# A decoder layer on one core: each pair of heads gets its transposes, its values and the next pair's scores in one place of the TensorE order, at nine steps

## The chip, the cores and the metric

One core of one Trainium2 chip runs the whole layer. The metric is the device time of one execution in microseconds (us), as the median of several executions. Before the change it is 853.51 us (three runs, 853.31 to 853.89).

## The reference, cut to what matters

The layer projects x (512 tokens, 1024 channels, float32) to queries, keys and values of three dilation groups with 8 heads of 64, to the input of a state-space branch and to gates. Each group attends causally over a window; the groups are merged by their softmax denominators, both branches are projected and gated, and a normalisation, a SwiGLU layer and another normalisation follow.

```python
q = apply_rope(q, pos); k = apply_rope(k, pos)
for g, (window, dilation) in enumerate(((128, 1), (512, 4), (2048, 16))):
    o_g, lse_g = dilated_group_attention(q[:, :, g], k[:, :, g], v[:, :, g], window, dilation)
    ...
wts = jax.nn.softmax(jnp.stack(lses, axis=0), axis=0)
attn = jnp.sum(wts[..., None] * jnp.stack(outs, axis=0), axis=0)
```

## The kernel before

Every dense product is made of three matmuls (`mm3`, lines 187 to 190): both operands are split in a high and a low part, and high by high, high by low and low by high are added in PSUM. The projection is a list of 56 tiles, `STEPS`; a tile is 24 matmuls of 128x128 by 128x512. Steps 4 to 7 make the values of group 0, 8 to 19 gates, 20 to 27 keys and queries of group 0, 28 to 39 group 1, 40 to 51 group 2 (k, q, v, k, q), and 52 to 55 the last four gate tiles. After them come the GLU (line 1035 on), the branch projections, the output projection and the feed-forward part.

Other work is put between these tiles by hand. `at_step(n, fn, ...)` files a call under a step, and `run_fill(n)` makes the calls filed there in the order of filing. A whole n is run in the middle of tile n (`mid`, between its 12th and 13th matmul), and n + 0.5 is run after tile n and after `w.release()`. That release emits the split of the next weights into the slot just freed: a cast to the high part on ScalarE (ACT, line 181), a subtraction for the low part on VectorE (DVE, line 182) and, every second time, the load of the next raw weights on SyncE (SP, line 118). Each engine works through its own instructions in the order in which the program emits them.

Attention is done for two kinds (0: group 0; 1: groups 1 and 2 together) and four pairs of heads each, in three functions:

- `attn_scores` (from line 785): the scores of four blocks of queries on TensorE (PE, line 799) into four PSUM banks; then for each block and head DVE masks them and takes the maximum (line 810) and ACT takes the exponential (line 812), into a tile `un` per block.
- `attn_turn` (line 815 on): for each block PE transposes `un` (line 822: 14 transposes for a pair of kind 0, 16 for kind 1) into a bank, and ACT copies it back into `un` (line 824).
- `attn_values` (line 826 on): PE multiplies `un` with the values (line 833: 28 matmuls for kind 0, 32 for kind 1), and ACT copies the result (lines 839 and 841).

Scores and values of neighbouring pairs stand together at nine places (`SCORES`), and the transposes stand alone at eight places in between (`WEIGHTS`). For the pairs that the prediction names: the transposes of pair 0 of kind 0 are at 32, its values and the scores of pair 1 at 33.5; the transposes of pair 3 of kind 1 are at 54, its values at 55.5.

Around the end of this stage `merge_weights` computes the weights of the merge from the maxima and denominators of all pairs: three small operations on DVE, an exponential on ACT (line 872), five small operations on DVE, a cast to `wt` on ACT (line 879) and a last subtraction on DVE. `merge_turn` transposes `wt` on PE (line 885). `split_y` splits the state-space result for the GLU: four operations on ACT (line 184) and four on DVE (line 185). None of the three issues a DMA. `merge_near` (SP and POOL) and `merge_sel` (DVE) keep their steps.

Of the kernel before, what the change touches and what calls it, by code (L numbers as in the profile page):

```python
# [44 lines left out]
NLAST = 4  # L45


SCORES = [[30, 33.5, 37, 40, 43.5], [43.5, 48.5, 51.5, 53, 55.5]]
WEIGHTS = [[32, 35.5, 38.5, 42], [45, 50, 52.5, 54]]

# [101 lines left out]
def emit(ctx, tc, i, out):  # L154
# [71 lines left out]
    for n in range(2, N_GLU, 2):  # L226
        kind, g, un, _ = STEPS[n]
# [699 lines left out]
    def at_step(n, fn, *a):  # L927
        fill.setdefault(n, []).append((fn, a))
# [37 lines left out]
        at_step(28 + rnd, ssm_out, rnd)  # L966
    at_step(30, turn_y)
    for kind in range(2):
        for j, n in enumerate(SCORES[kind]):
            if j > 0:  # L970
                at_step(n, attn_values, kind, j - 1)
            if j < NPAIR:
                at_step(n, attn_scores, kind, j)
                at_step(WEIGHTS[kind][j], attn_turn, kind, j)
    xn = []
    pending = []

# [12 lines left out]
    at_step(43, merge_near, 0)  # L990
    at_step(45, merge_near, 1)
    at_step(52, merge_sel)
    at_step(54.5, split_y)
    at_step(54, merge_weights)
    at_step(55.5, merge_turn)
    for hp in range(NPAIR):
        at_step((58, 59, 60, 61)[hp], merge_pair, hp)

# [11 lines left out]
    for n in range(4, N_GLU):  # L1010
        kind, g, un, c = STEPS[n]
# [345 lines left out]
def build(inputs):  # L1357
    import concourse.bacc as bacc

    a = {k: np.asarray(v) for k, v in inputs.items()}  # L1360
    arrays = {f"in_{k}": np.ascontiguousarray(v) for k, v in {**layout(a), **constants()}.items()}
    nc = bacc.Bacc("TRN2", target_bir_lowering=False, num_devices=1)
    aps = {k[3:]: nc.dram_tensor(k, v.shape, mybir.dt.from_np(v.dtype), kind="ExternalInput").ap()
           for k, v in arrays.items()}
    out = nc.dram_tensor("out_dram", (S, D), F32, kind="ExternalOutput").ap()
    with tile.TileContext(nc) as tc:
        with ExitStack() as ctx:
            with tc.manual_schedule():
                emit(ctx, tc, aps, out)
    return nc, arrays  # L1370
# [8 lines left out]
```

## Time and profile before

| | |
|---|---|
| median of the runs | 853.51 us (853.31 to 853.89) |
| the profiled execution | 853.05 us, of which its span is 851.3 us |
| PE busy | 842.9 us (99%) |
| ACT busy | 302.8 us (36%) |
| DVE busy | 485.4 us (57%) |

The profile shows one execution. The span runs from the first to the last instruction, and 1.75 us lie around it. Ends of matmuls are modelled, so what a matmul takes of PE's time is read from one start to the next.

### The profile page before, as it was taken

To read this page: it belongs to the slowest core of one execution; us is meant where nothing else is said; L and a number is where in the kernel's file an instruction comes from. 1 tells how busy PE (TensorE), PEld (TensorE's weight loads), DVE (VectorE), ACT (ScalarE), POOL (GpSimd) and SP (SyncE) were. 2 spreads that over 40 slices of the span, in tenths; PEclk is the share of its full clock that TensorE was granted. 3 is DMA by queue.
4 is the path that set the end of the run, shared out by engine and by line. 5 is a ranking of instruction groups with operands and counts; after the bars stand their busy time and mean duration, and the time that the engine had idled before them with its cause. 6 is when DMAs were issued, how large, how long until landed. Compare 5 with 4: busy or idle time off the path is not lost.

```text
span 851.3 us, 11306 instructions
## 1 busy us (share of the span) xinstructions
PE 842.9 (99%) x4576; PEld 702.2 (82%) x4576; DVE 485.4 (57%) x949; ACT 302.8 (36%) x481; POOL 25.4 (3%) x27
## 2 busy tenths in 40 slices
PE   9999999999999999999999999999999999999996
PEld 7888888888888888888888898888888888888885
DVE  7977899964666446347785854433434434222237
ACT  6873221264344444643241332222222222211101
POOL 0000000000000000000000500000000000000005
PEclk9999999999999999999999999999999999999999
DMA  9822421424121321121642142222222222422203
GB/s 331 208 99 88 124 99 54 145 79 170 50 99 50 102 100 50 50 95 55 247 146 102 50 149 99 99 99 99 99 100 99 93 89 89 136 94 97 97 0 100
DMA packets 24580, 90.06 MB, mean 106 GB/s; under 512 B 6352, under 2 KB 11216, under 8 KB 15440
## 3 DMA queue, kind: packets, MB, share of 16 engines
q1 hardware_dynamic: 22752, 86.59, 29.7%
q10 hardware_dynamic: 1776, 2.74, 0.9%
q8 instruction: 36, 0.59, 0.3%
q14 instruction: 16, 0.13, 0.0%
HBM read 84.87 MB, written 4.46 MB: 105 GB/s over the span
## 4 chain that ended last, share of the span: by engine, by line
PE 98%; DMA 1%; DVE 0%; SPq 0%; issue 0%; DVEq 0%; ACT 0%
PE fg L188 9%; PE fg L190 9%; PE fg L189 9%; PE dn L190 4%; PE dn L189 4%; PE dn L188 4%; PE pg L188 4%; PE pg L189 3%; PE pg L190 3%; PE pv L188 3%; PE pk L188 3%; PE pq L188 3%; PE pv L189 3%; PE pv L190 3%; PE pq L190 3%; PE pk L190 3%
## 5 line engine op out<-in xcount | busy, mean ns | idle before, releaser
L182 DVE TENSOR_TENSOR wlo<-raw,whi 128x1024 fp32r<-128x1024 f32 x134 | 164.3, 1227 | 192.5 <-ACT whi L181 192.5
L181 ACT CAST whi<-raw 128x1024 fp32r<-128x1024 f32 x134 | 140.1, 1047 | 234.9 <-PE dn L190 73.4
L188 PE MATMUL fg<-hh,whi 128*128 128x512 f32 (+1 forms) x376 | 141.4, 376 | 0.0
L189 PE MATMUL fg<-hl,whi 128*128 128x512 f32 (+1 forms) x376 | 141.3, 376 | 0.0
L190 PE MATMUL fg<-hh,wlo 128*128 128x512 f32 (+1 forms) x376 | 141.3, 376 | 0.0
L189 PEld LDWEIGHTS fg<-hl,whi 128*128 128x128 f32 x376 | 70.8, 188 | 12.9
L190 PEld LDWEIGHTS fg<-hh,wlo 128*128 128x128 f32 x376 | 70.8, 188 | 12.9
L188 PEld LDWEIGHTS fg<-hh,whi 128*128 128x128 f32 x376 | 70.8, 188 | 12.6
L189 PE MATMUL dn<-wlo,ff 128*128 128x512 f32 x168 | 65.4, 389 | 0.0
L190 PE MATMUL dn<-whi,ff 128*128 128x512 f32 x168 | 65.4, 389 | 0.0
L188 PE MATMUL dn<-whi,ff 128*128 128x512 f32 x168 | 65.4, 389 | 0.0
L188 PE MATMUL pg<-x_hi,whi 128*128 128x512 f32 x128 | 50.5, 395 | 0.0
L184 ACT ACTIVATE ff<-fth 128x512 fp32r<-128x512 f32 x22 | 14.0, 634 | 102.8 <-DVE fth L321 102.8
L190 PE MATMUL pg<-x_hi,wlo 128*128 128x512 f32 x128 | 49.9, 390 | 0.0
L189 PE MATMUL pg<-x_lo,whi 128*128 128x512 f32 x128 | 49.9, 390 | 0.0
L321 DVE TENSOR_TENSOR fth<-fth,fg 128x512 f32<-128x512 f32 x22 | 15.1, 688 | 56.8 <-PE fg L190 56.7
L188 PE MATMUL pq<-x_hi,whi 128*128 128x512 f32 x96 | 37.9, 395 | 0.0
L188 PE MATMUL pk<-x_hi,whi 128*128 128x512 f32 x96 | 37.8, 394 | 0.0
L190 PE MATMUL pq<-x_hi,wlo 128*128 128x512 f32 x96 | 37.5, 390 | 0.0
L190 PE MATMUL pk<-x_hi,wlo 128*128 128x512 f32 x96 | 37.4, 390 | 0.0
L189 PE MATMUL pq<-x_lo,whi 128*128 128x512 f32 x96 | 37.4, 390 | 0.0
L189 PE MATMUL pk<-x_lo,whi 128*128 128x512 f32 x96 | 37.4, 390 | 0.0
(256 smaller groups left out, 1460.4 us busy)
## 6 DMA issues: line engine op xcount, KB each, us to landing
raw<-in_w_in SPq DMA_DIRECT2D x26, 1024.0 KB, 4.8
raw<-in_w_gu SPq DMA_DIRECT2D x22, 1024.0 KB, 4.7
raw<-in_w_dn SPq DMA_DIRECT2D x11, 1024.0 KB, 4.7
raw<-in_w_br SPq DMA_DIRECT2D x4, 1024.0 KB, 4.8
raw<-in_w_out SPq DMA_DIRECT2D x4, 1024.0 KB, 4.7
raw<-in_w_glu SPq DMA_DIRECT2D x2, 1024.0 KB, 4.7
xn<-in_x SPq DMA_DIRECT2D x2, 1024.0 KB, 7.9
out_dram<-hn SPq DMA_DIRECT2D x12, 128.0 KB, 2.3
```

The lines of the kernel that those rows point to most:

```text
L181: act.copy(hi, src)
L182: dve.tensor_tensor(lo, src, hi.bitcast(F32), op=ALU.subtract)
L184: act.mul(hi, src, scale)
L188: pe.matmul(dst, a[0], b[0], start=first, stop=False)
L189: pe.matmul(dst, a[0], b[1], start=False, stop=False)
L190: pe.matmul(dst, a[1], b[0], start=False, stop=last)
L321: eng.tensor_tensor(o, a, b, op=op)
```

## The change

`SCORES` and `WEIGHTS` become one list, `TURNS`. At each of its steps the transposes of the pair before, its values and the scores of the next pair are emitted one behind the other. All steps of the list are whole, so every place lies in the middle of a tile. `split_y`, `merge_weights` and `merge_turn` move by half a step to a step.

```diff
-SCORES = [[30, 33.5, 37, 40, 43.5], [43.5, 48.5, 51.5, 53, 55.5]]
-WEIGHTS = [[32, 35.5, 38.5, 42], [45, 50, 52.5, 54]]
+TURNS = [[30, 33, 36, 39, 43], [43, 48, 51, 53, 55]]
...
     for kind in range(2):
-        for j, n in enumerate(SCORES[kind]):
+        for j, n in enumerate(TURNS[kind]):
             if j > 0:
+                at_step(n, attn_turn, kind, j - 1)
                 at_step(n, attn_values, kind, j - 1)
             if j < NPAIR:
                 at_step(n, attn_scores, kind, j)
-                at_step(WEIGHTS[kind][j], attn_turn, kind, j)
...
     at_step(52, merge_sel)
-    at_step(54.5, split_y)
-    at_step(54, merge_weights)
-    at_step(55.5, merge_turn)
+    at_step(53.5, split_y)
+    at_step(54.5, merge_weights)
+    at_step(55, merge_turn)
```

## Rows read from the trace of the kernel before

**Rows 1.** The page, its first two parts: busy time of the engines, then the granted clock in 40 slices.
```profile
PE 842.9 (99%) x4576; PEld 702.2 (82%) x4576; DVE 485.4 (57%) x949; ACT 302.8 (36%) x481; POOL 25.4 (3%) x27
...
PEclk9999999999999999999999999999999999999999
```
**Rows 2.** The page's chain that ended last, by engine.
```profile
PE 98%; DMA 1%; DVE 0%; SPq 0%; issue 0%; DVEq 0%; ACT 0%
```
**Rows 3.** Who PE waited for, whole span: total us, times, longest.
```profile
PE warm_b L267 <- DVE warm L263: 1.1, 1, 1.1
PE pu L595 <- ACT wuh L181: 0.3, 1, 0.3
```
**Rows 4.** PE in order of time around the transposes at step 32: start, length, instruction.
```profile
198.21 0.39 PE L190 MATMUL pk<-x_hi,wlo 128*128 128x512 f32 x1
198.44 1.69 PE L822 MATMUL t<-ident,un 128*128 128x128 f32 x14
199.89 0.48 PE L188 MATMUL pk<-x_hi,whi 128*128 128x512 f32 x1
...
200.43 0.39 PE L190 MATMUL pk<-x_hi,wlo 128*128 128x512 f32 x1
```
**Rows 5.** PE around the values and scores at step 33.5, the same columns.
```profile
207.92 0.39 PE L190 MATMUL pk<-x_hi,wlo 128*128 128x512 f32 x1
208.24 1.75 PE L833 MATMUL o<-un,v 128*64 128x128 f32 x28
209.91 1.79 PE L799 MATMUL s<-k,q 64*128 64x128 f32 x16
211.63 0.50 PE L188 MATMUL pk<-x_hi,whi 128*128 128x512 f32 x1
```
**Rows 6.** PE around the transposes at step 54 (kind 1).
```profile
356.66 0.40 PE L190 MATMUL pg<-x_hi,wlo 128*128 128x512 f32 x1
356.90 1.91 PE L822 MATMUL t<-ident,un 128*128 128x128 f32 x16
358.56 0.47 PE L188 MATMUL pg<-x_hi,whi 128*128 128x512 f32 x1
...
359.11 0.40 PE L190 MATMUL pg<-x_hi,wlo 128*128 128x512 f32 x1
```
**Rows 7.** PE from the first matmul of tile 55 on: its 1st, its 13th, its last, and the place at 55.5.
```profile
361.41 0.39 PE L188 MATMUL pg<-x_hi,whi 128*128 128x512 f32 x1
...
364.13 0.39 PE L188 MATMUL pg<-x_hi,whi 128*128 128x512 f32 x1
...
366.94 1.97 PE L833 MATMUL o<-un,v 128*64 128x128 f32 x32
368.84 0.66 PE L885 MATMUL wt<-ident,wt 128*128 128x128 f32 x4
```
**Rows 8.** PE at step 53: the values of a pair of kind 1, then the scores.
```profile
347.43 1.97 PE L833 MATMUL o<-un,v 128*64 128x128 f32 x32
349.33 2.06 PE L799 MATMUL s<-k,q 64*128 64x128 f32 x32
```
**Rows 9.** ACT in order of time: the copies at step 32, four merged in one row; in brackets the idle time before and what ended it.
```profile
198.91 2.00 ACT L824 COPY un<-t 128x256 f32<-128x256 f32 x4 [1.46 <-PE t L822]
```
**Rows 10.** ACT from step 54 to the first GLU tile.
```profile
357.59 2.05 ACT L824 COPY un<-t 128x512 f32<-128x512 f32 x4 [0.94 <-PE t L822]
359.50 0.29 ACT L872 ACTIVATE dm<-dm 128x64 f32<-128x64 f32 x1
361.03 0.24 ACT L879 CAST wt<-dm 128x64 fp32r<-128x64 f32 x1 [1.24 <-DVE dm L321]
361.61 0.69 ACT L912 ACTIVATE gt<-pg,bgate 128x512 f32<-128x512 f32 x1 [0.34 <-PE pg L190]
362.20 1.04 ACT L181 CAST whi<-raw 128x1024 fp32r<-128x1024 f32 x1
```
**Rows 11.** DVE in the same stretch.
```profile
357.83 0.18 DVE L321 TENSOR_TENSOR mg<-near_st,st 128x32 f32<-128x32 f32 x1
...
358.16 0.18 DVE L321 TENSOR_TENSOR dm<-mg,st 128x32 f32<-128x32 f32 x1
359.82 0.19 DVE L321 TENSOR_TENSOR mg<-dm,near_st 128x32 f32<-128x32 f32 x1 [1.48 <-ACT dm L872]
...
363.27 1.23 DVE L182 TENSOR_TENSOR wlo<-raw,whi 128x1024 fp32r<-128x1024 f32 x1 [1.74 <-ACT whi L181]
364.41 2.49 DVE L185 SCALAR_TENSOR_TENSOR ych<-ych,yh 128x512 fp32r<-128x512 f32 x4
```
**Rows 12.** ACT near the start, and PE's one wait for it there.
```profile
7.24 0.62 ACT L181 CAST wuh<-wu_raw 128x512 fp32r<-128x512 f32 x1
```
**Rows 13.** PE there.
```profile
7.92 0.98 PE L595 MATMUL pu<-x_hi,wuh 128*128 128x512 f32 x3 [0.29 <-ACT wuh L181]
```
**Rows 14.** ACT after the scores of step 53: the end of the last exponential and the next gate tile's evacuation.
```profile
354.96 0.19 ACT L812 ACTIVATION_READ_ACCUMULATOR un<-un,st 128x1 f32 x1
355.05 0.67 ACT L912 ACTIVATE gt<-pg,bgate 128x512 f32<-128x512 f32 x1
```
**Rows 15.** Busy time by stretch: stretch, its length, PE busy (instructions), PEld, DVE, ACT and POOL likewise, mean granted clock, DMA share, GB/s.
```profile
340.00:345.00 5.00, 5.00 (x32) 4.39 (x31) 1.52 (x3) 3.71 (x11) 0.00 (x0) 1.00 0.00 0
844.20:851.30 7.10, 0.04 (x1) 0.00 (x0) 3.78 (x8) 0.00 (x0) 2.02 (x2) 0.72 0.42 127
```

## The prediction

> **What bounds the kernel now.** I read the page first. PE is busy for 842.9 of 851.3 us at the full granted clock [rows 1], and the chain that ended last is PE for 98% [rows 2]. The waits of PE settle what that means: over the whole span PE waited for another engine twice, 1.1 and 0.3 us, both near the start [rows 3]. So through the stage that is changed PE works without a pause, and everything on ACT, DVE and the DMA queues is hidden. Only two things can move the time: fewer or cheaper instructions on PE, or a new wait of PE. The timeline of PE around a few places shows what a place costs in itself, and those of ACT and DVE show when the data of a place would be ready.
>
> The profiled execution took 853.05 us, 0.46 below the median of the runs, 853.51. The sum is made against the former and carried over to the latter. About 0.2%, or 1.7 us, is what a measurement of this kernel can tell from no change.
>
> **The change part by part.** No matmul, transpose or copy is added or removed; their order changes. Dense matmuls follow each other every 0.227 us (12 in 2.72, from 361.41 to 364.13) [rows 7].
>
> *Eight places fewer.* Around the transposes of step 32 two L190 starts are 2.22 us apart, of which three dense pitches are 0.68; 14 transposes thus cost 1.54 [rows 4]. At step 54 it is 2.45 less 0.68, or 1.77 for 16 [rows 6]. Two transposes more cost 0.23 by these sums and 0.21 by the starts (1.45 and 1.66), so one costs 0.105 to 0.115, and what a place adds to its transposes lies between nothing and 0.07. I take 0.03, the middle: eight places save 0.24 us (0 to 0.56).
>
> *The way into the values.* From the last dense matmul to the first of the values 0.32 us pass, 0.09 over the pitch [rows 5]; into the transposes 0.23, nothing over [rows 4]. After the change the values follow transposes instead. No row shows that passage. The nearest is the reverse: 32 values last 1.90 us to the next start, whether scores follow [rows 8] or the transposes of the merge [rows 7], so going between whole and half array is charged to transposes as to others. I take 0.09 as now, a change of 0; the bounds are -0.09 (as dense to transposes) and +0.09 (twice), times eight -0.72 to +0.72. [...]
>
> *The copies that the values now wait for.* Before, 1.5 tiles lay between transposes and values; now none. At step 32 the four copies end 2.47 us after the first transpose (198.44; 198.91 plus 2.00) [rows 4, 9], at step 54 2.74 after it (356.90; 357.59 plus 2.05) [rows 6, 10]. PE gets to the fourth block's values at 1.45 + 0.09 + 20/28 of 1.67 = 2.73 for kind 0 [rows 4, 5], and at 1.66 + 0.09 + 3/4 of 1.90 = 3.18 for kind 1 [rows 6, 8]. PE starts 0.06 us after an ACT result that it waits for (7.24 plus 0.62; 7.92) [rows 12, 13]. The copies are then in time, with 0.20 and 0.38 us to spare; earlier blocks have more. I cost the seven places at 33, 36, 39, 43, 48, 51 and 53 at nothing. The cover is that ACT is idle in the middle of a tile: in tile 55, begun at 361.41, evacuation and cast are over at 363.24, 0.89 before its middle [rows 7, 10], and other tiles have only the cast there. The exponentials end 7.7 us after the values began (347.43; 355.15) [rows 8, 14], long before the next place two tiles on. If that cover were gone, each us that ACT is late beyond the spare is a us of PE.
>
> *The place at 55.* Here the cover is gone. `merge_weights` now stands at 54.5, ahead of these copies in ACT's queue; before, at 54, it stood behind them. Its cast to `wt` waits for a chain of DVE, and the copies wait behind it. Counted from the middle of tile 55 (364.13 [rows 7]): DVE is through with the low part at 364.41, +0.28; three small operations take 0.51 (357.83 to 358.34) [rows 11]; handing over 0.06; the exponential until DVE goes on 0.32 (359.50 to 359.82); five operations until the cast 1.21 (to 361.03); the cast 0.24 [rows 10, 11]. Together 2.62, where the first copy would start at 0.69. Four copies, 2.05, end at 4.67; PE goes on to the fourth block at 4.73 instead of 3.18, which is 1.55 later. Neighbouring ACT operations overlap by some 0.1 (the exponential starts at 359.50, the copies end at 359.64), so I take 1.5, with 1.2 and 2.0 as ends for the same chain a few tenths shorter or longer. PE waits for nothing later, so all of it reaches the end.
>
> *The other moves.* `split_y` at 53.5 needs DVE for 2.49 us [rows 11] and ACT for as many operations. Counted from the first transpose of step 53, the exponentials end at 1.75 + 7.7 = 9.5, evacuation and cast 1.6 later at 11.1 (lengths as in tile 55 [rows 10]), DVE's low part and its share of `split_y` at about 14.8. Tile 54 ends at 1.75 + 2 x 1.95 + 2.72 + 5.44 = 13.8, and DVE is wanted 1.86 after that (363.27 against 361.41 [rows 7, 11]), at 15.7, so the chain above starts on time. `merge_turn` at 55 needs the last DVE operation of the chain, over 1.5 us before PE gets there. These three issue no DMA. SP's weight loads hang on DVE's low parts, which come at most about 1 us later behind the exponentials of a mid-tile place, against three slots of weights ahead. `merge_near` on SP and POOL follows the scores of its kind as before. Nothing.
>
> Sum: 1.5 - 0.24 = +1.26 us. Against the profiled execution that gives 854.3, against the median 854.8.
>
> **Rivals.** *Copies late at the other seven places (slower).* The spare time of 0.20 (four places of kind 0) and 0.38 (three of kind 1) is short. It decides if PE needs the copy not 0.06 but over 0.31 us ahead, since 4 x 0.11 = 0.44 more passes 0.2%. At 0.6 the price is 4 x 0.40 + 3 x 0.22 = 2.3, giving 857.0. For it: 0.06 is one wait of a dense matmul, ahead of small ones that pass at 0.06 each (28 in 1.67 [rows 5]). Against it: it is a wait between the same two engines.
>
> [...]
>
> *The wait at 55 does not come, and the way into the values is free.* Then -0.24 - 0.72 = -0.96, or 852.5, still within 0.2%; for a faster verdict more than that would have to be found. Against it stands the order of ACT's queue.
>
> **How the numbers follow.** The forecast has 0.67; its own ends are -0.56 - 0.72 + 1.2 = -0.1 and 2.0 + 0.72 = 2.7, so 853.4 to 856.2, and I put 0.12 of it above 1.7. Late copies have 0.20, the clock 0.04, no wait 0.09 with 0.02 of it below -1.7. Faster is thus 0.02, within 0.2% 0.55 + 0.07 = 0.62, slower 0.12 + 0.20 + 0.04 = 0.36. The range goes from 853.2 to 857.0 and leaves out the clock, most of the last case and the worst of the late copies, some 0.15.
>
> **What would show it.** The list of PE's waits should gain one row: the values (line 833 before) waiting for the copies of ACT, once, about 1.5 us, at step 55, with ACT's cast to `wt` just ahead of those copies. At the other seven places the values should follow the transposes without idle time. [...] A time under 852 us or over 857 would mean a cost that I have not seen.

## The result, and the profile after

The changed kernel takes 854.76 us (median of 20 runs, 854.09 to 855.63), the kernel before in the same runs 853.61 us (20 runs, 853.09 to 854.16). The ratio is 1.0014, with a 95% interval of 1.0007 to 1.0020: 1.15 us more, clear of no change, and within the 0.2% that the prediction took as its bound. That bound was too wide: with 20 runs of each kernel 0.14% can be told from nothing. The range (853.2 to 857.0) holds it, and the forecast, 854.8, lies 0.04 us off.

The profiled execution took 854.82 us with a span of 853.0. It answers to [rows 3] with this list of PE's waits (engine and tile that waited, who ended it: total us, times, longest). All line numbers after the change are lower by one.

```profile
PE o L832 <- ACT un L823: 1.2, 1, 1.2
PE warm_b L266 <- DVE warm L262: 1.1, 1, 1.1
PE pu L594 <- ACT wuh L180: 0.5, 1, 0.5
PE kb L550 <- issue: 0.4, 1, 0.4
```

The first row is new, and it is the only one that belongs to the changed stage: the values waited for a copy once, by this list, for 1.2 us. The last two lie in the first 63 us, where both kernels run the same code; by the starts of PE's matmuls they put the changed kernel 0.65 us behind at that point (0.34 from the first loads on, 0.32 in line 550). The span's difference of 1.7 us is therefore not all the change's. The medians don't have this difference of two single executions in them.

PE at step 55, in order of time, answers to [rows 7]:

```profile
362.75 1.91 PE L821 MATMUL t<-ident,un 128*128 128x128 f32 x16
365.83 2.12 PE L832 MATMUL o<-un,v 128*64 128x128 f32 x32 [1.18 <-ACT un L823]
367.88 0.66 PE L884 MATMUL wt<-ident,wt 128*128 128x128 f32 x4
```

ACT in the same stretch answers to [rows 10]:

```profile
360.81 1.04 ACT L180 CAST whi<-raw 128x1024 fp32r<-128x1024 f32 x1
363.56 0.26 ACT L871 ACTIVATE dm<-dm 128x64 f32<-128x64 f32 x1 [1.72 <-DVE dm L320]
365.05 0.24 ACT L878 CAST wt<-dm 128x64 fp32r<-128x64 f32 x1 [1.23 <-DVE dm L320]
365.20 2.04 ACT L823 COPY un<-t 128x512 f32<-128x512 f32 x4
```

The transposes start at 362.75, and their copies at 365.20, directly behind the cast to `wt` that had waited 1.23 us for DVE. From the transposes' start to that of the values 3.08 us pass, where a place without a wait takes 1.84 (below), and the 32 values take 2.05 instead of 1.90. Together 1.39 us. The 0.15 has the same cause: the values come in four blocks of 8, and each block starts 0.05 us after the end of its own copy. The copies end 0.49 us apart, where the later blocks without a wait follow each other in 0.44, and the last block takes 0.05 longer.

Now a place without a wait, first of kind 0 (step 33), then of kind 1 (step 48), on PE:

```profile
204.53 1.69 PE L821 MATMUL t<-ident,un 128*128 128x128 f32 x14
206.15 1.75 PE L832 MATMUL o<-un,v 128*64 128x128 f32 x28
207.83 1.79 PE L798 MATMUL s<-k,q 64*128 64x128 f32 x16
...
307.02 1.91 PE L821 MATMUL t<-ident,un 128*128 128x128 f32 x16
308.85 1.97 PE L832 MATMUL o<-un,v 128*64 128x128 f32 x32
310.75 2.06 PE L798 MATMUL s<-k,q 64*128 64x128 f32 x32
```

and ACT's copies there:

```profile
205.00 2.00 ACT L823 COPY un<-t 128x256 f32<-128x256 f32 x4 [2.11 <-PE t L821]
...
307.65 2.05 ACT L823 COPY un<-t 128x512 f32<-128x512 f32 x4 [1.63 <-PE t L821]
```

No row of PE has idle time before it. The copies end 2.47 and 2.68 us after the first transpose, and ACT was idle before them (the brackets). What a place costs can be read from starts alone: the time from the start of the dense matmul ahead of it to that of the fourth dense matmul behind it, less 0.227 for each of these four. Added up this way ("by the starts" from here on), the attention's places cost 1.26 us more than before: 1.39 more at step 55, and 0.13 less at the seven others, some 0.02 each.

### The profile page after: what moved, and what is told of

The parts are those of the page before. It is cut to its first block, busy times and chain, and to the rows that moved or that the text cites. A ratio compares the mean times of both kernels' runs of the same rounds, so it can differ in the third digit from the quotient of the medians.

```text
span 853.0 us, 11273 instructions
## 1 busy us (share of the span) xinstructions
PE 842.9 (99%) x4576; PEld 702.9 (82%) x4576; DVE 485.7 (57%) x949; ACT 303.0 (36%) x481; POOL 25.4 (3%) x27
## 3 DMA queue, kind: packets, MB, share of 16 engines
q10 hardware_dynamic: 1776, 2.74, 0.9%
## 4 chain that ended last, share of the span: by engine, by line
PE 98%; DMA 1%; DVE 0%; ACT 0%; issue 0%; SPq 0%; DVEq 0%; ACTq 0%
PE fg L187 9%; PE fg L188 9%; PE fg L189 9%; PE dn L189 4%; PE dn L187 4%; PE dn L188 4%; PE pg L187 3%; PE pg L189 3%; PE pg L188 3%; PE pq L187 3%; PE pv L187 3%; PE pk L187 3%; PE pv L188 3%; PE pq L189 3%; PE pv L189 3%; PE pq L188 3%
```

## The experiments

Seven kernels were run, four beside one set of runs of the kernel before (853.53 us), three beside another (853.62).

### 1. The merge's weights behind the copies

```diff
             if j > 0:
                 at_step(n, attn_turn, kind, j - 1)
+                if n == 55:
+                    at_step(n, merge_weights)
                 at_step(n, attn_values, kind, j - 1)
...
-    at_step(54.5, merge_weights)
-    at_step(55, merge_turn)
+    at_step(55.5, merge_turn)
```

> The merge's weights stand at step 55 between the transposes and the values, so behind the four copies in ACT's queue, and the merge's own transposes at 55.5; all else as changed. My theory (PE waits at 55 only because the copies queue behind the cast of the merge's weights): the wait of 1.2 us goes, the copies end 2.7 us after the first transpose, before PE needs the last of them at 3.2; the time falls by 1.4 us against the changed kernel to about 853.5, the same as before within 0.2 us (0.1 to 0.2 less for the cheaper places). Rival (the values directly behind the transposes cost the wait in themselves, whatever ACT's order): the wait stays, 854.8.

Measured: 853.74 us against 853.53, ratio 1.0002 (0.9994 to 1.0011), which leaves out the rival's 854.8. PE has no wait in the stage. At step 55 ACT now has:

```profile
363.27 2.05 ACT L823 COPY un<-t 128x512 f32<-128x512 f32 x4 [1.59 <-PE t L821]
365.19 0.29 ACT L871 ACTIVATE dm<-dm 128x64 f32<-128x64 f32 x1
366.71 0.25 ACT L878 CAST wt<-dm 128x64 fp32r<-128x64 f32 x1 [1.24 <-DVE dm L320]
```

and PE:

```profile
362.58 1.91 PE L821 MATMUL t<-ident,un 128*128 128x128 f32 x16
364.42 1.97 PE L832 MATMUL o<-un,v 128*64 128x128 f32 x32
```

The cast still waits 1.24 us for DVE, but nothing stands behind it that PE needs. The merged place itself costs nothing; that rival is out. What the cheaper places save (0.09 us by the starts, with one place more for the merge's transposes) is below what the runs can tell.

### 2. The three merge steps put back

```diff
-    at_step(53.5, split_y)
-    at_step(54.5, merge_weights)
-    at_step(55, merge_turn)
+    at_step(54.5, split_y)
+    at_step(54, merge_weights)
+    at_step(55.5, merge_turn)
```

> The three merge steps go back to where they were (splitting y at 54.5, the weights at 54, the merge's transposes at 55.5), the nine places stay. My theory (what counts is what ACT has ahead of the copies, not the weights as such): the cast of the weights holds ACT until the end of tile 54, evacuation and cast follow, then four operations of the split of y until about 1.8 us after the first transpose of step 55; the copies end at 3.8, PE waits about 0.6 us. About 854.1, 0.5 above before. Rival (the chain of the weights alone makes the wait): no wait, 853.5. Rival (the place itself): 854.8.

Measured: 853.66 us, ratio 1.0003 (0.9994 to 1.0012). The time leaves out the last expectation (854.8) and can't tell the first two (854.1 and 853.5) apart. PE's list of waits has no row in this stage, which is what the first rival said. ACT's rows and the starts of PE say more:

```profile
359.49 0.24 ACT L878 CAST wt<-dm 128x64 fp32r<-128x64 f32 x1 [1.23 <-DVE dm L320]
359.64 0.68 ACT L911 ACTIVATE gt<-pg,bgate 128x512 f32<-128x512 f32 x1
360.22 1.04 ACT L180 CAST whi<-raw 128x1024 fp32r<-128x1024 f32 x1
361.16 2.19 ACT L183 ACTIVATE yh<-ych 128x512 fp32r<-128x512 f32 x4
363.25 2.03 ACT L823 COPY un<-t 128x512 f32<-128x512 f32 x4
```

ACT runs without a pause from the cast to `wt` to the copies, so it is the queue, now with other work in it, that holds them. They start 1.29 us after the first transpose (361.96), not 1.8 as I expected: I had added the lengths of ACT's operations, and neighbours overlap by about 0.1 each. Each block of values starts 0.05 us behind its copy, as in the changed kernel, and by the starts the place loses 0.23 us (0.08 ahead of the values, 0.15 in them), in gaps too small for the list. Direction as in the theory, size a little over a third of the 0.6 that I gave.

### 3. Merged places at the old half steps

```diff
-TURNS = [[30, 33, 36, 39, 43], [43, 48, 51, 53, 55]]
+TURNS = [[30, 33.5, 37, 40, 43.5], [43.5, 48.5, 51.5, 53, 55.5]]
```

and the three merge steps as in experiment 2.

> The transposes join the values where the values were before: steps 33.5, 37, 40, 43.5, 48.5, 51.5, 53 and 55.5, four of them behind a tile and its cast of weights, with the merge steps as before. My theory: at 33.5, 43.5, 48.5 and 51.5 the copies start behind the cast, about 1 us instead of 0.5 to 0.7 after the first transpose, and still just make it (0 to 0.05 us of wait each); at 55.5 ACT first has the evacuation and the cast of the gate tile and the copies end 3.8 us after the first transpose, where PE needs the last at 3.2: one wait of 0.6 us. About 854.1, 0.5 above before. Rival (a merged place is free only in the middle of a tile): waits of 0.4 us or more at each of the five half steps, 855.5 or more.

Measured: 854.33 us against 853.53, ratio 1.0008 (0.9999 to 1.0017). The interval just reaches no change and leaves out the rival's 855.5; what was lost where is read from the trace. PE's list of waits has one row in the stage, at 55.5:

```profile
365.12 1.91 PE L821 MATMUL t<-ident,un 128*128 128x128 f32 x16
367.49 2.12 PE L832 MATMUL o<-un,v 128*64 128x128 f32 x32 [0.45 <-ACT un L823]
369.53 0.65 PE L884 MATMUL wt<-ident,wt 128*128 128x128 f32 x4
```

for copies that stood behind the gate tile's evacuation and cast:

```profile
365.32 0.69 ACT L911 ACTIVATE gt<-pg,bgate 128x512 f32<-128x512 f32 x1 [1.55 <-PE pg L189]
365.91 1.04 ACT L180 CAST whi<-raw 128x1024 fp32r<-128x1024 f32 x1
366.85 2.05 ACT L823 COPY un<-t 128x512 f32<-128x512 f32 x4
```

The place lost 0.65 us, the two of kind 0 behind a tile (33.5 and 43.5) 0.09 each in their last block, those at 48.5 and 51.5 nothing. The model of the spare time holds to 0.05 us here, and a merged place need not lie in the middle of a tile: it needs ACT free.

### 4. The copies late at all eight places

```diff
             n = 128 * len(ks)
+            for _ in range(2 if blk == 0 else 0):
+                act.copy(un[:, :, 0:n], tb[:, :, 0:n])
             act.copy(un[:, :, 0:n], tb[:, :, 0:n])
```

> The changed kernel with the first block's copy done three times over at all eight places, so that the other copies come 0.35 us later for kind 0 and 0.96 for kind 1. My theory (the fourth block's copy has 0.3 us to spare for kind 0 and 0.5 for kind 1, and each us beyond is a us of PE): waits of about 0.05 us at 33, 36, 39 and 43, of 0.45 at 48, 51 and 53, and 0.96 more at 55, in all 2.5 us more than the changed kernel, about 857.3. Rival (PE needs a copy well ahead of its matmul, so the spare is smaller by 0.2 or more): 1.4 us more than that, 858.7 or above. Rival (later work of PE takes up the wait): 854.8 to 855.3.

Measured: 861.72 us (4 runs, 860.84 to 862.10) against 853.53, ratio 1.0095 (1.0081 to 1.0109). That is 4.4 us above my figure. It lies in the open range of the first rival, but not for its reason: two things were wrong in my figure, and neither is the spare time. (The added lines make the values L834 and the last copies L825 here and in experiments 6 and 7.) First, the delay: copies upon the same tile don't overlap, as ACT's rows at step 48 show, behind PE's (two copies take 1.20 and the third starts 0.62 behind the second, where different blocks follow each other in 0.48).

```profile
308.34 1.91 PE L821 MATMUL t<-ident,un 128*128 128x128 f32 x16
310.85 2.12 PE L834 MATMUL o<-un,v 128*64 128x128 f32 x32 [0.60 <-ACT un L825]
...
308.97 1.20 ACT L824 COPY un<-t 128x512 f32<-128x512 f32 x2 [1.63 <-PE t L821]
310.21 2.05 ACT L825 COPY un<-t 128x512 f32<-128x512 f32 x4
```

The copies thus came 0.64 (kind 0) and 1.24 us (kind 1) later, not 0.35 and 0.96. At step 48 they end 3.92 us after the first transpose (308.34), and the fourth block of values starts 0.05 behind them, at 3.97. In the changed kernel it starts at 3.20. The block itself takes 0.05 longer than without a wait, and the place lost 0.83. PE thus needs a copy no more than 0.05 us ahead, which rules out the first rival's reason. By the starts, the four places of kind 0 lost 0.42 to 0.47 each, those of kind 1 0.83 to 0.89. Second, step 55, where PE waited 2.42 us:

```profile
366.59 1.91 PE L821 MATMUL t<-ident,un 128*128 128x128 f32 x16
370.92 3.55 PE L834 MATMUL o<-un,v 128*64 128x128 f32 x32 [2.42 <-ACT un L825]
374.40 0.69 PE L886 MATMUL wt<-ident,wt 128*128 128x128 f32 x4
```

The values took 3.48 us instead of 2.05. The busy time by stretch (as in [rows 15]; the granted clock is the number behind POOL) says why:

```profile
368.30:370.90 2.60, 0.20 (x2) 0.00 (x0) 0.76 (x3) 1.93 (x5) 0.00 (x0) 1.00 0.89 350
370.90:374.40 3.50, 3.48 (x32) 3.15 (x33) 0.00 (x0) 1.43 (x3) 0.00 (x0) 0.53 0.08 26
374.40:377.00 2.60, 2.60 (x15) 2.22 (x14) 0.69 (x1) 0.59 (x1) 0.00 (x0) 0.98 0.00 0
```

The granted clock was 1.00 through the wait, 0.53 in the mean of the 3.50 us right behind it, and 0.98 in the 2.60 us after that. Step 55 lost 2.71 us over the changed kernel, 1.25 by the wait and 1.43 in the values, at the lower clock. All eight places together are 7.1, and 6.96 lie between the medians (861.72 and 854.76).

### 5. ACT's order alone, in the kernel before

```diff
+    at_step(54, merge_weights)
     for kind in range(2):
         for j, n in enumerate(SCORES[kind]):
...
-    at_step(54, merge_weights)
```

> The kernel before with one thing changed: at step 54 the merge's weights are emitted ahead of the transposes, so that the four copies queue behind the same cast as in the changed kernel, while the values stay at 55.5. My theory (the wait takes both, copies behind the cast and values directly behind the transposes): the copies come some 2.5 us later than before and end around 362.2, nearly 5 us before the values start; PE waits for nothing new; 853.5, as before. Rival (ACT's order alone costs the time, by what it delays of evacuations and casts): 854.7.

Measured: 853.90 us against 853.62, ratio 1.0003 (0.9994 to 1.0012). The interval ends at 854.6, just below the rival's 854.7. PE has no new wait in the stage, and by the starts its places cost the same as before, to 0.01 us in all. The copies come late on ACT and nobody needs them yet:

```profile
357.90 1.91 PE L822 MATMUL t<-ident,un 128*128 128x128 f32 x16
367.94 1.97 PE L833 MATMUL o<-un,v 128*64 128x128 f32 x32
...
360.87 0.24 ACT L879 CAST wt<-dm 128x64 fp32r<-128x64 f32 x1 [1.23 <-DVE dm L321]
361.02 2.04 ACT L824 COPY un<-t 128x512 f32<-128x512 f32 x4
362.94 0.72 ACT L912 ACTIVATE gt<-pg,bgate 128x512 f32<-128x512 f32 x1
```

The copies end at 363.06 and the values start at 367.94. The wait thus takes both: the copies behind the cast, and the values right behind the transposes.

### 6 and 7. One and two more copies at step 55 alone

```diff
             n = 128 * len(ks)
+            for _ in range(1 if (kind, hp, blk) == (1, 3, 0) else 0):
+                act.copy(un[:, :, 0:n], tb[:, :, 0:n])
```

and the same with `range(2 ...)`.

> The changed kernel with the first block's copy of step 55 done twice. A copy upon the same tile took 0.62 us from start to start in the run with all places, so the copies come 0.62 later and PE waits 1.8 us instead of 1.2 at that place. My theory (a us of wait is a us of time while the granted clock holds): +0.6 against the changed kernel, 855.4, clock 1.00 throughout. [...]

> The changed kernel with the first block's copy of step 55 done three times, and all other places as changed: the wait there becomes 2.4 us as in the run with all places. My theory (that wait alone makes the clock fall): the granted clock is at half for some 3.4 us after the wait, the values take 3.5 us instead of 2.05; +2.7 against the changed kernel, 857.5. Rival (the fall came of the eight waits together): the clock holds, +1.25, 856.0.

Measured: 855.28 us with one (ratio to before 1.0021, 1.0013 to 1.0030), 856.10 with two (5 runs, 855.70 to 857.75; 1.0033, 1.0020 to 1.0045). The waits of PE are 1.8 and 2.4 us. With one more, a us of wait was a us of time: +0.6 by the starts at step 55, as expected. With two, I expected the clock to fall, and in the profiled execution it did not:

```profile
362.26 1.91 PE L821 MATMUL t<-ident,un 128*128 128x128 f32 x16
366.59 2.12 PE L834 MATMUL o<-un,v 128*64 128x128 f32 x32 [2.42 <-ACT un L825]
...
366.60:370.00 3.40, 3.40 (x40) 2.88 (x41) 0.67 (x1) 1.99 (x4) 0.00 (x0) 1.00 0.06 19
```

The last row is the busy time by stretch, with the clock at 1.00. The same 2.42 us of wait left it at 1.00 here, and 0.53 followed it in experiment 4. Of the five runs, four are 855.70 to 856.31, which is the rival's figure, and one is 857.75 with a mean clock of 0.996 instead of 0.997 to 0.998, which is close to my figure. That this one had the fall fits its time, but it has no profile. In experiment 4 three of the four runs have 0.996 too, and the fourth, with 0.998, is the shortest (860.84); no run of any other kernel here is under 0.997. Whether the seven other waits make the fall likelier in experiment 4 stays open.

## Why the prediction was right

**The sum.** By the starts the change costs 1.26 us, and the prediction's sum is 1.26. That the two agree so closely is luck: the loss at step 55 was put 0.11 too high, the saving of the places 0.11 too high as well, and the two errors cancel. What was right is the path and the wait, and each term to about a tenth of a us.

**The bound.** PE without a pause through the stage, and everything else hidden: experiment 5 shows it from the other side, since copies that start 3.1 us after the first transpose (361.02 against 357.90) instead of 0.69 cost nothing where PE doesn't want them yet.

**Eight places fewer.** Mis-sized: 0.24 us were put down, the starts give 0.02 for each of the seven places without a wait, 0.13 in all (the eighth place's share is inside the 1.39 of step 55). The bounds (0 to 0.56) held it. The two-decimal rows could not say more than 0 to 0.07 for a place, and the middle of that was too high.

**The way into the values.** Right. From transposes to values 1.62 us for 14 and 1.84 for 16 leave 0.11 for a transpose and 0.09 for the passage, as from a dense matmul to the values before. What makes up the 0.09 no run shows. In PE's rows the shape changes three times for a pair, before and after (128*128 to 128*64, to 64*128, and back), and merging saved no more than the 0.02.

**The seven places at nothing.** Right. The copies end 2.47 and 2.68 us after the first transpose (2.47 and 2.74 expected), and the fourth block starts at 2.76 and 3.20 (2.73 and 3.18 expected). Less the 0.05 of handing over, 0.24 and 0.46 us were to spare. The price put on the rival, us for us beyond the spare time, holds in experiments 3 and 4, with another 0.05 for a last block that waited. Two details were off, without effect on the forecast. The spare time of 0.20 and 0.38 already has the 0.06 taken off, so the rival's figures count it twice: PE would have to need the copies over 0.37 us ahead (not 0.31) to pass 0.2%, and at 0.6 the price is 4 x 0.34 + 3 x 0.16 = 1.8, giving 856.6 (not 857.0). And 1.5 tiles lay between transposes and values at six of the eight places only; from 45 to 48.5 there were 3.5, from 52.5 to 53 half a tile.

**Step 55.** Right in its place and its cause, and in its size to 0.11: the first copy was put at 2.62 us after the first transpose and came at 2.45, the last end at 4.67 and came at 4.49, the loss at 1.5 and was 1.39. Experiments 1 and 5 each take away one half of the cause, and the loss is gone both times.

**The clock.** Right that it would most likely hold in this kernel, as far as its one profile shows: the wait of 1.2 us directly behind 16 transposes left it at 1.00.

```profile
364.50:365.80 1.30, 0.15 (x2) 0.00 (x0) 0.71 (x3) 0.75 (x3) 0.00 (x0) 1.00 0.68 246
365.80:367.90 2.10, 2.07 (x33) 1.69 (x33) 0.00 (x0) 1.44 (x3) 0.00 (x0) 1.00 0.73 308
```

The 0.04 for a fall was my estimate, and no run of this kernel shows one (the clocks of its 20 runs are 0.997 to 0.999). Where it did fall, in experiment 4, to 0.53 over 3.50 us, it cost 1.43 us.

## What to carry to other kernels

When a producer and its consumer on the bounding engine are moved together, read what the engine in between has in its queue at that very point: an instruction there that waits for a third engine passes its wait on to everything emitted behind it, as ACT's cast did here, which waited 1.23 us for DVE: the copies behind it came 2.45 us after the first transpose instead of 0.69 (experiment 1), and PE waited 1.18 us for them. A merged place cost nothing here where the copies had 0.24 us or more to spare, and that spare time was worked out to a tenth of a us from a few rows of PE and ACT before the change. Fewer places gained 0.02 us each, so in this kernel the list of places is worth arranging for the queues and not for their number.

## What the runs showed that I had not expected

The granted clock averaged 0.53 over the 3.50 us behind a wait of 2.42 us (16 transposes just ahead of it) in one profiled execution (experiment 4), and stayed at 1.00 through and behind a wait of 2.42 us at the same place in another (experiment 7). Through 1.2 us it stayed at 1.00 too, and the profiled execution with 1.8 us has a mean of 0.999. Two ACT copies of 128x512 upon the same tile stand 0.62 us apart, upon different ones 0.48. And 32 values that come right behind a wait take 2.05 us instead of 1.90, so that a wait costs PE more than the list shows: the blocks behind the first follow their own copies, in gaps that the list leaves out.
